# First loads of a hybrid decoder trunk: pieces of 256 and 768 weight columns between the input chunks, and the first norm's squares behind all operands

## The chip, the cores and the metric

The kernel runs on one core of one Trainium2 chip, as one launch. The metric is the device time of an execution in microseconds (us); lower is better. All times below are from the kernel's own runs or from the trace of one profiled execution of it.

In the profile PE is TensorE's matmuls and PEld its weight loads, DVE is VectorE, ACT is ScalarE, POOL is GpSimd, and SP is the queue that issues nearly all loads. L165 is line 165 of the kernel before.

## The reference

Two layers over x of 512 tokens and 1024 features, in float32. Layer 0 has a causal convolution module, layer 1 differential attention; each is followed by a SwiGLU feed-forward (2816 wide) and a gated per-layer embedding. What the change touches is the start of layer 0:

```python
def rms_norm(x, g):
    y = x * rsqrt(mean(x * x, axis=-1, keepdims=True) + EPS)
    return y * g

def conformer_conv(x, w_pw1, b_pw1, dw_w, dw_b, ln_g, ln_b, w_pw2, b_pw2):
    a = x @ w_pw1 + b_pw1                                 # (512, 2048)
    u = a[..., :1024] * sigmoid(a[..., 1024:])
    u = depthwise_causal_conv(u, dw_w, width=31) + dw_b   # each feature by itself
    u = silu(layer_norm(u, ln_g, ln_b))
    return u @ w_pw2 + b_pw2

u = rms_norm(h, conv_norm_g[0])
h = h + conformer_conv(u, ...)
```

## The kernel before

Activations lie transposed: 8 chunks `h[0]` to `h[7]` of 128 features (partitions) by 512 tokens, 256 KB each. A weight tile is 128 x 1024: the 8 input chunks' blocks of 128 x 128 side by side, for 128 output features; 512 KB each.

Every product runs as three matmuls (`mm3`, L163 to L167) on operands split in two: a high part, cast to the reduced-precision matmul type on ScalarE, and a low part, the rest, subtracted on VectorE. `weight()` (L146) takes the next tile from `wts` with a load on the SP queue into one of two `wraw` buffers, casts it into one of four `whi` (L158) and subtracts into one of four `wlo` (L160). A load into a `wraw` buffer waits until the tile before the last one has been cast and subtracted. In the text the tiles are called w0, w1, w2 and so on, in the order of their loads.

The norm is a class with two steps for a chunk. `operands(c)` makes the two matmul operands of h[c] times the gain (`A`: ScalarE at L179, VectorE at L180). `squares(c)` adds the chunk's squares into `acc` (ScalarE at L201 and L204, VectorE at L205). The scale by the root mean square is not in the operands: it is multiplied into the results. For that, `columns()` sums `acc` over the partitions on TensorE (L211), `rsqrt_cols` makes the reciprocal root of it on VectorE and GpSimd (L228, L230), `diagonal` spreads that over the identity (L235), a matmul with ones turns it into rows (L245), and ScalarE copies these to SBUF as `rb` (L220).

The convolution stage runs over 8 output chunks c. Each takes two weight tiles, a gate half and a value half, and each `half(w)` sums 8 input chunks x 3 matmuls = 24 matmuls in one accumulator. The accumulators (`mm`) are four PSUM buffers taken in turn: chunk 0 takes the first two, chunk 1 the other two, and chunk 2 needs the first again. VectorE reads an accumulator at L482 (gate) and L488 (value), times `rb`, and by that frees it. The depthwise convolution runs beside this on VectorE, GpSimd and, for some chunks in a phased layout, on TensorE (`pe_taps`).

At the start the SP queue loads w0 in two halves of 512 columns with h[0] between them, then w1's first half, h[1], w1's second half, h[2], and h[3] to h[7], the depthwise weights, w2, the side input `p` of layer 0 and w3. ScalarE and VectorE do the operands of a chunk and right behind them its squares. Nine matmuls on constants (`WARM`, L140) stand ahead of everything on TensorE.

The order on each engine is made by the framework's scheduler at build time, from the program's order and a model of the times; on the chip each engine runs its list in that order, and a wait holds up all that stands behind it.

Of the kernel before, what the change touches and what calls it, by code (L numbers as in the profile page):

```python
# [13 lines left out]
F32R = mybir.dt.float32r  # L14
AF = mybir.ActivationFunctionType
ALU = mybir.AluOpType
# [4 lines left out]
P = 128  # L21
S = 512
D = 1024
NC = D // P
# [22 lines left out]


SHIFT = 1
WARM = 9  # L50
ALONE = (7,)
CUTS = 2

# [39 lines left out]
def trunk(ctx, tc, xT, pT, wts, diag, dww, vec, rel, onehot, lamv, out):  # L93
    nc = tc.nc
    V, A, G, T = nc.vector, nc.scalar, nc.gpsimd, nc.tensor
# [7 lines left out]
    def sb(shape, tag, bufs, dt=F32):  # L103
        uid[0] += 1
        return pool.tile(shape, dt, tag=tag, name=f"{tag}_{uid[0]}", bufs=bufs)
# [10 lines left out]
    f = lambda ap: ap.bitcast(F32)  # L116
# [6 lines left out]
    def col(name, i=0):  # L123
        a, _ = VEC[name]
        return vt[:, a + i : a + i + 1]
# [12 lines left out]
    t = tp()  # L138
    for k in range(WARM):
        T.matmul(t[:, 0:P], ident, ones, start=True, stop=True)  # L140
# [2 lines left out]
    wnext = [0]  # L143
    loaded = [None]

    def weight(n=1024, pieces=1, between=(), eng=V, after=None, behind=None):  # L146
        i = wnext[0]
        wnext[0] += 1
        raw = sb([P, 1024], "wraw", 2)
        hi = sb([P, 1024], "whi", 4, F32R)  # L150
        lo = sb([P, 1024], "wlo", 4, F32R)
        for k in range(pieces):
            cut = slice(k * n // pieces, (k + 1) * n // pieces)
            loaded[0] = nc.sync.dma_start(raw[:, cut], wts[i, :, cut])
            if k < len(between):
                between[k]()
            with tc.issue_after(behind.ins) if behind else nullcontext():
                A.copy(hi[:, cut], raw[:, cut])  # L158
            with tc.issue_after(after.ins) if after else nullcontext():
                eng.tensor_tensor(lo[:, cut], raw[:, cut], f(hi[:, cut]), ALU.subtract)  # L160
        return hi, lo

    def mm3(acc, a, b, first, last):  # L163
        (ah, al), (bh, bl) = a, b
# [11 lines left out]
    h = [sb([P, S], f"h{c}", 1) for c in range(NC)]  # L176

    def split_scaled(src, scale, hi, lo):
        A.activation(hi, src, AF.Copy, scale=scale)  # L179
        V.scalar_tensor_tensor(lo, src, scale, f(hi), ALU.mult, ALU.subtract)  # L180

    class Norm:

# [9 lines left out]
        def operands(self, c):  # L193
            hi = sb([P, S], f"A{2 * c}", 1, F32R)
            lo = sb([P, S], f"A{2 * c + 1}", 1, F32R)
            split_scaled(h[c], col(self.g, c), hi, lo)
            self.u.append((hi, lo))

        def squares(self, c):
            if c == 0:  # L200
                A.activation(self.acc, h[c], AF.Square)  # L201
            else:
                sq = wk()
                self.square = A.activation(sq, h[c], AF.Square)  # L204
                self.last = self.eng.tensor_tensor(self.acc, self.acc, sq, ALU.add)  # L205
# [42 lines left out]

    norm = Norm("conv_g", V)
    def load(c):  # L250
        return lambda: nc.sync.dma_start(h[c], xT[c])

    w0 = weight(pieces=2, between=(load(0),))
    norm.operands(0)
    w1 = weight(pieces=2, between=(load(1), load(2)))
    pair_loads = [loaded[0]]
    pairs = [(w1, w0)]
    for c in range(3, NC):
        load(c)()
    dwt = sb([P, NC * KW], "C4", 2)  # L260
    nc.sync.dma_start(dwt, dww)
    for c in range(1, NC):
        norm.operands(c)
    pairs.append((weight(), weight())[::-1])
    pair_loads.append(loaded[0])
    for c in range(NC):
        norm.squares(c)

    def pfeatures(layer, parts):
        for k, (hi, lo) in enumerate(parts):  # L270
# [329 lines left out]
    norm = Norm("ffn_g0")  # L600
# [8 lines left out]
    def ffn(norm, after, space):  # L609
# [102 lines left out]
        def strassen(i):  # L712

            w = operands(i)

            def product(acc, name):
                for k in range(4):
                    mm3(acc, wpart(w[name], k), comb[name][k], k == 0, k == 3)

            one, two, three, four = sc(), mm(), mm(), tp()  # L720
            t, e, g = wk(), big(), big()
            first, second = slice(0, H2), slice(H2, S)
            product(one[:, first], 1)
            A.copy(t[:, first], one[:, first])
            A.mul(t[:, second], one[:, first], -1.0)
            product(three[:, first], 5)
            product(three[:, second], 7)
            product(two[:, first], 2)
            product(two[:, second], 6)
            V.tensor_tensor(e, two, t, ALU.add)  # L730
            V.tensor_tensor(
                g.rearrange("p (a s) -> p a s", a=2), three.rearrange("p (a s) -> p a s", a=2),
                e[:, second].unsqueeze(1).to_broadcast([P, 2, H2]), ALU.add,
            )
            V.tensor_tensor(e[:, second], three[:, second], g[:, first], ALU.add)
            product(four[:, second], 4)
            V.tensor_tensor(g[:, second], four[:, second], g[:, second], ALU.add)
            product(four[:, first], 3)
            V.tensor_tensor(g[:, first], four[:, first], g[:, first], ALU.subtract)
            return e, g  # L740
# [91 lines left out]
    norm = Norm("attn_g")  # L832
# [202 lines left out]
    def stage_o(hd):  # L1035
        t = tp()
        for i in range(4):
            T.transpose(t[:, i * P : (i + 1) * P], osb[hd][:, i * P : (i + 1) * P], ident)
        hi = sb([P, S], f"A{2 * hd}", 1, F32R)
        lo = sb([P, S], f"A{2 * hd + 1}", 1, F32R)  # L1040
        split_scaled(t, gains[:, 1:2], hi, lo)
        ot[hd] = (hi, lo)
# [9 lines left out]
    def take(n):  # L1052
        got, stages[:n] = [s for _, s in stages[:n]], []
        return got

    waiting = None
    for what, at, pace in QKV:
        ws = slab(GLO if what == "q" and at > 0 else 0, P * at[1] if what == "v" else S)
        for tb in range(4):
            if (what, at, tb) == ("v", (6, 2), 0):  # L1060
                ph = pfeatures(1, [both(sb([P, 2, S], t, 1, F32R)) for t in ("B0", "B1")])
            between = take(3 * pace[tb])
# [23 lines left out]
    for m in range(NC):  # L1086
        if m % 4 == 0:
            w = weight()
# [9 lines left out]
    norm = Norm("ffn_g1")  # L1098
# [149 lines left out]
```

## Time and profile before

| | |
|---|---|
| time, median of 3 runs | 1251.86 us (1250.25 to 1252.58) |
| time of the profiled execution | 1249.44 us |
| its span in the trace | 1247.7 us |
| instructions in the trace | 18537 |
| read from HBM | 151.91 MB |

A row of the timeline or of the waits gives start and duration in us, the engine, the source line, the operation, the tile written and the tiles read, and, in brackets, how long the engine had been idle and what ended it. Rows that follow each other on one engine can be merged (x2); then the duration is their sum. The page's busy time of TensorE holds pipelined matmuls, so it shows where TensorE waits, not how well it works.

### The profile page before, as it was taken

How to read it: one execution, taken by the hardware profiler on the slowest of the kernel's cores; microseconds unless marked ns; L12 is line 12 of the kernel's file. 1: busy time of each engine (PE TensorE's matmuls, PEld its weight loads, DVE VectorE, ACT ScalarE, POOL GpSimd, SP SyncE). 2: the span in 40 equal slices, each digit the busy share in tenths (PEclk: the TensorE clock that was granted, in tenths of full speed). 3: DMA queues.
4: the chain of work that ended last, by engine and by line, in shares of the span. 5: the costliest groups of instructions: out<-in, count | busy, mean ns of one | idle time of the engine just before them, and what ended most of it. 6: DMA issues, size and time to landing. Idle time of an engine off the chain costs nothing.

```text
span 1247.7 us, 18537 instructions
## 1 busy us (share of the span) xinstructions
PE 1234.6 (99%) x7152; PEld 1083.8 (87%) x7152; DVE 885.6 (71%) x1422; ACT 614.1 (49%) x1023; POOL 264.4 (21%) x231
## 2 busy tenths in 40 slices
PE   9999999999999999999999999999999999999998
PEld 7888788898899889988888988878898999899887
DVE  6998765965688568677667879546964598458665
ACT  6743454542355325355557778635432355235441
POOL 2852522000000000042526644131000000000030
PEclk9999999999999999999999999999999999999999
DMA  8666223464466444243232215122654466443241
GB/s 300 201 195 189 67 73 113 125 172 127 127 176 179 128 125 124 64 142 95 85 111 76 75 45 159 62 87 82 185 141 131 119 175 185 130 120 110 76 136 68
DMA packets 60598, 158.39 MB, mean 127 GB/s; under 512 B 6452, under 2 KB 11060, under 8 KB 60509
## 3 DMA queue, kind: packets, MB, share of 16 engines
q1 hardware_dynamic: 53776, 136.99, 34.6%
q0 software_dynamic: 4608, 16.78, 7.9%
q10 hardware_dynamic: 2124, 3.43, 0.9%
q8 instruction: 56, 0.92, 0.3%
q14 instruction: 34, 0.27, 0.1%
HBM read 151.91 MB, written 4.21 MB: 125 GB/s over the span
## 4 chain that ended last, share of the span: by engine, by line
PE 95%; DVE 3%; ACT 1%; issue 1%; DMA 0%; SPq 0%; DVEq 0%; ACTq 0%
PE mm L165 25%; PE mm L166 25%; PE mm L167 25%; PE tp L166 2%; PE tp L167 2%; PE tp L165 2%; PE sc L371 2%; PE sc L166 1%; PE sc L167 1%; PE sc L165 1%; PE mm L1012 1%; PE mm L371 1%; PE tp L998 1%; PE sc L979 1%; PE mm L327 1%
## 5 line engine op out<-in xcount | busy, mean ns | idle before, releaser
L166 PE MATMUL mm<-A,whi 128*128 128x512 f32 (+1 forms) x904 | 311.4, 346 | 1.1 <-DVE A L576 0.9
L167 PE MATMUL mm<-A,whi 128*128 128x512 f32 (+1 forms) x904 | 310.2, 343 | 0.0
L165 PE MATMUL mm<-A,wlo 128*128 128x512 f32 (+1 forms) x904 | 306.8, 345 | 3.2 <-DVE wlo L160 1.7
L158 ACT CAST whi<-wraw 128x1024 fp32r<-128x1024 f32 (+2 forms) x150 | 151.1, 1014 | 226.2 <-PE mm L167 94.1
L160 DVE TENSOR_TENSOR wlo<-wraw,whi 128x1024 fp32r<-128x1024 f32 (+2 forms) x147 | 186.0, 1268 | 64.5 <-ACT whi L158 64.0
L165 PEld LDWEIGHTS mm<-A,wlo 128*128 128x128 f32 x904 | 171.4, 190 | 24.3 <-ACT A L179 2.3
L166 PEld LDWEIGHTS mm<-A,whi 128*128 128x128 f32 x904 | 171.5, 190 | 23.0 <-DVE A L576 1.8
L167 PEld LDWEIGHTS mm<-A,whi 128*128 128x128 f32 x904 | 171.5, 190 | 20.7 <-issue 1.4
L167 PE MATMUL mm<-B,whi 128*128 128x512 f32 x368 | 143.4, 391 | 0.0
L166 PE MATMUL mm<-B,whi 128*128 128x512 f32 x368 | 143.4, 391 | 0.0
L165 PE MATMUL mm<-B,wlo 128*128 128x512 f32 x368 | 141.4, 392 | 0.0
L685 POOL DMA_DIRECT2D C<-in_wts x32 | 28.1, 878 | 512.4 <-DVE h L796 178.9
L205 POOL TENSOR_TENSOR acc<-acc,wk 128x512 f32<-128x512 f32 x35 | 56.2, 1606 | 219.0 <-ACT wk L204 113.3
L167 PEld LDWEIGHTS mm<-B,whi 128*128 128x128 f32 x368 | 69.2, 188 | 14.9
L165 PE MATMUL mm<-whi,A 128*128 128x512 f32 (+1 forms) x224 | 81.5, 367 | 0.0
L166 PE MATMUL mm<-wlo,A 128*128 128x512 f32 (+1 forms) x224 | 81.5, 366 | 0.0
L166 PEld LDWEIGHTS mm<-B,whi 128*128 128x128 f32 x368 | 69.2, 188 | 14.2
L165 PEld LDWEIGHTS mm<-B,wlo 128*128 128x128 f32 x368 | 69.1, 188 | 14.1
L167 PE MATMUL mm<-whi,A 128*128 128x512 f32 (+1 forms) x224 | 81.2, 364 | 0.0
L796 DVE TENSOR_TENSOR h<-mm,h 128x512 f32<-128x512 f32 x48 | 33.0, 687 | 64.7 <-PE mm L167 64.7
L230 POOL TENSOR_TENSOR r<-v,mhalf 128x8 f32<-128x8 f32 (+1 forms) x31 | 46.7, 1505 | 104.7 <-DVE v L228 100.3
L678 DVE TENSOR_TENSOR wlo<-wraw,whi 128x1024 fp32r<-128x1024 f32 x32 | 39.2, 1224 | 31.3 <-ACT whi L677 31.1
(269 smaller groups left out, 2618.5 us busy)
## 6 DMA issues: line engine op xcount, KB each, us to landing
wraw<-in_wts SPq DMA_DIRECT2D x162, 512.0 KB, 3.6
C<-in_wts SPq DMA_DIRECT2D x32, 512.0 KB, 4.5
C<-in_wts POOLq DMA_DIRECT2D x32, 512.0 KB, 6.2
bias<-in_wts SPq DMA_DIRECT2D x32, 256.0 KB, 3.4
wraw<-in_wts SPq DMA_DIRECT2D x16, 384.0 KB, 3.1
D<-in_diag SPq DMA_DIRECT2D x22, 256.0 KB, 4.6
C<-in_diag SPq DMA_DIRECT2D x16, 256.0 KB, 4.7
h<-in_xT SPq DMA_DIRECT2D x8, 256.0 KB, 5.1
```

Of the source, the lines that this page charges most:

```text
L158: A.copy(hi[:, cut], raw[:, cut])
L160: eng.tensor_tensor(lo[:, cut], raw[:, cut], f(hi[:, cut]), ALU.subtract)
L165: T.matmul(acc, al, bh, start=first, stop=False)
L166: T.matmul(acc, ah, bl, start=False, stop=False)
L167: return T.matmul(acc, ah, bh, start=False, stop=last)
L205: self.last = self.eng.tensor_tensor(self.acc, self.acc, sq, ALU.add)
L230: last_pow[0] = G.tensor_tensor(r[:, :n], v[:, :n], mhalf[:, :n], ALU.pow)
L327: last_tap[0] = T.matmul(acc, dg[:, j % 4], ups[c][:, j : j + S], start=(j == 0), stop=(j == PE_TAPS[c] - 1))
L371: last_tap[0] = T.matmul(acc[:, g * P : (g + 1) * P], w, ups[c][:, g, LEAD - m : LEAD - m + P], start=(m == 0), stop=(m == LAGS - 1),)
L678: V.tensor_tensor(lo, raw, f(hi), ALU.subtract)
L685: nc.gpsimd.dma_start(q, wts[i + 2].rearrange("p (a s) -> p a s", a=2), accum_op=ALU.add)
L796: V.tensor_tensor(h[m], acc, h[m], ALU.add)
```

## The change

The code of `weight()` is taken apart into `opened()`, which takes the buffers, and `fetch()`, which loads, casts and subtracts a range of columns. w0 and w1 are opened together, and the first loads are: 256 columns of w0, h[0], 256 columns of w1, h[1], the other 768 of w0, h[2], the other 768 of w1, then h[3] to h[7]. A first piece of 256 columns is what input chunks 0 and 1 multiply. All squares of the first norm are ordered behind the cast of the last operand. One matmul on constants is left out (`WARM` 9 to 8). The arithmetic is the same.

```diff
--- before.py
+++ after.py
@@ -47,7 +47,7 @@
 
 
 SHIFT = 1
-WARM = 9
+WARM = 8
 ALONE = (7,)
 CUTS = 2
 
@@ -143,22 +143,23 @@
     wnext = [0]
     loaded = [None]
 
-    def weight(n=1024, pieces=1, between=(), eng=V, after=None, behind=None):
+    def opened():
         i = wnext[0]
         wnext[0] += 1
-        raw = sb([P, 1024], "wraw", 2)
-        hi = sb([P, 1024], "whi", 4, F32R)
-        lo = sb([P, 1024], "wlo", 4, F32R)
-        for k in range(pieces):
-            cut = slice(k * n // pieces, (k + 1) * n // pieces)
-            loaded[0] = nc.sync.dma_start(raw[:, cut], wts[i, :, cut])
-            if k < len(between):
-                between[k]()
-            with tc.issue_after(behind.ins) if behind else nullcontext():
-                A.copy(hi[:, cut], raw[:, cut])
-            with tc.issue_after(after.ins) if after else nullcontext():
-                eng.tensor_tensor(lo[:, cut], raw[:, cut], f(hi[:, cut]), ALU.subtract)
-        return hi, lo
+        return i, sb([P, 1024], "wraw", 2), sb([P, 1024], "whi", 4, F32R), sb([P, 1024], "wlo", 4, F32R)
+
+    def fetch(w, cut, eng=V, after=None, behind=None):
+        i, raw, hi, lo = w
+        loaded[0] = nc.sync.dma_start(raw[:, cut], wts[i, :, cut])
+        with tc.issue_after(behind.ins) if behind else nullcontext():
+            A.copy(hi[:, cut], raw[:, cut])
+        with tc.issue_after(after.ins) if after else nullcontext():
+            eng.tensor_tensor(lo[:, cut], raw[:, cut], f(hi[:, cut]), ALU.subtract)
+
+    def weight(n=1024, **how):
+        w = opened()
+        fetch(w, slice(0, n), **how)
+        return w[2:]
 
     def mm3(acc, a, b, first, last):
         (ah, al), (bh, bl) = a, b
@@ -176,8 +177,9 @@
     h = [sb([P, S], f"h{c}", 1) for c in range(NC)]
 
     def split_scaled(src, scale, hi, lo):
-        A.activation(hi, src, AF.Copy, scale=scale)
+        cast = A.activation(hi, src, AF.Copy, scale=scale)
         V.scalar_tensor_tensor(lo, src, scale, f(hi), ALU.mult, ALU.subtract)
+        return cast
 
     class Norm:
 
@@ -193,8 +195,8 @@
         def operands(self, c):
             hi = sb([P, S], f"A{2 * c}", 1, F32R)
             lo = sb([P, S], f"A{2 * c + 1}", 1, F32R)
-            split_scaled(h[c], col(self.g, c), hi, lo)
             self.u.append((hi, lo))
+            return split_scaled(h[c], col(self.g, c), hi, lo)
 
         def squares(self, c):
             if c == 0:
@@ -248,23 +250,28 @@
 
     norm = Norm("conv_g", V)
     def load(c):
-        return lambda: nc.sync.dma_start(h[c], xT[c])
-
-    w0 = weight(pieces=2, between=(load(0),))
-    norm.operands(0)
-    w1 = weight(pieces=2, between=(load(1), load(2)))
+        nc.sync.dma_start(h[c], xT[c])
+
+    w0, w1 = opened(), opened()
+    start, rest = slice(0, 2 * P), slice(2 * P, NC * P)
+    for c, (w, cut) in enumerate(((w0, start), (w1, start), (w0, rest))):
+        fetch(w, cut)
+        load(c)
+        norm.operands(c)
+    fetch(w1, rest)
     pair_loads = [loaded[0]]
-    pairs = [(w1, w0)]
+    pairs = [(w1[2:], w0[2:])]
     for c in range(3, NC):
-        load(c)()
+        load(c)
     dwt = sb([P, NC * KW], "C4", 2)
     nc.sync.dma_start(dwt, dww)
-    for c in range(1, NC):
-        norm.operands(c)
+    for c in range(3, NC):
+        cast = norm.operands(c)
     pairs.append((weight(), weight())[::-1])
     pair_loads.append(loaded[0])
-    for c in range(NC):
-        norm.squares(c)
+    with tc.issue_after(cast.ins):
+        for c in range(NC):
+            norm.squares(c)
 
     def pfeatures(layer, parts):
         for k, (hi, lo) in enumerate(parts):
```

The scheduler places what follows anew. Three places are shown, each before and after; the kernel after has other line numbers (L158 is L155 there, L160 L157, L165 to L167 are L166 to L168, L179 is L180, L201 L203, L204 L206, L211 L213, L228 L230, L235 L237, L245 L247, L279 L286 and L482 L489).

The first place is ScalarE at the end of the first norm's operands: `A` are operands, `wk` squares, `wth` and `wtl` the side input, and `whi` behind `wraw` the weight w2. Before:

```order
L179 ACTIVATE A_33_143<-h_12_91,vec_63 128x512
L204 ACTIVATE wk_180<-h_12_91 128x512
L179 ACTIVATE A_35_147<-h_13_92,vec_63 128x512
L204 ACTIVATE wk_183<-h_13_92 128x512
L179 ACTIVATE A_37_151<-h_14_93,vec_63 128x512
L204 ACTIVATE wk_186<-h_14_93 128x512
L158 CAST whi_156<-wraw_155 128x1024
L279 CAST wth_256<-B_66_260 128x512
L279 CAST wtl_258<-B_66_260 128x512
```

Now:

```order
L180 ACTIVATE A_37_150<-h_14_92,vec_63 128x512
L203 ACTIVATE acc_93<-h_7_85 128x512
L206 ACTIVATE wk_167<-h_8_86 128x512
L206 ACTIVATE wk_170<-h_9_87 128x512
L206 ACTIVATE wk_173<-h_10_88 128x512
L206 ACTIVATE wk_176<-h_11_89 128x512
L286 CAST wth_255<-B_66_259 128x512
L286 CAST wtl_257<-B_66_259 128x512
L206 ACTIVATE wk_179<-h_12_90 128x512
L155 CAST whi_155<-wraw_154 128x1024
L206 ACTIVATE wk_182<-h_13_91 128x512
```

The squares were between the operands and w2 came right behind the last of them; now six squares and the side input stand between the last operand and w2's cast.

The second place is TensorE around the column sums of the norm, which write `tp` from `acc`. Before (the first rows are the end of chunk 0, `mm_286` is the gate half of chunk 1):

```order
L166 MATMUL mm_227<-A_38_152,whi_110 128x512
L167 MATMUL mm_227<-A_37_151,whi_110 128x512
L211 MATMUL tp_216<-ones_70,acc_94 128x1 x4
L165 MATMUL mm_286<-A_19_105,wlo_157 128x512
L166 MATMUL mm_286<-A_20_106,whi_156 128x512
```

Now (`mm_285` is the gate half of chunk 1, `mm_311` its value half):

```order
L167 MATMUL mm_285<-A_38_151,whi_155 128x512
L168 MATMUL mm_285<-A_37_150,whi_155 128x512
L213 MATMUL tp_215<-ones_70,acc_93 128x1 x4
L166 MATMUL mm_311<-A_22_104,wlo_162 128x512
L167 MATMUL mm_311<-A_23_105,whi_161 128x512
```

The column sums have moved behind 24 more matmuls, a whole half. The matmul that spreads the diagonal (L245) stood within chunk 1's value half, behind 8 of its 24 matmuls; now it stands behind all of them, and the next matmul is the first of chunk 2, `mm_420`.

The third place is what ScalarE and VectorE do around `rb` and the first read of an accumulator (`whi_275` and `wlo_276` before, `whi_274` and `wlo_275` now, are w4; the next tiles are w5 and w6). ScalarE before:

```order
L158 CAST whi_162<-wraw_161 128x1024
L158 CAST whi_275<-wraw_274 128x1024
L220 COPY rb_252<-tp_253 128x512
L158 CAST whi_281<-wraw_280 128x1024
L483 ACT_TABLE_LOAD
```

ScalarE now, down to the copy of `rb`, with two more casts ahead of it:

```order
L155 CAST whi_161<-wraw_160 128x1024
L155 CAST whi_274<-wraw_273 128x1024
L155 CAST whi_280<-wraw_279 128x1024
L155 CAST whi_409<-wraw_408 128x1024
L222 COPY rb_251<-tp_252 128x512
```

VectorE before, from the root's first step (`v`) on:

```order
L228 TENSOR_SCALAR v_56_221<-tp_216 128x4
L235 TENSOR_TENSOR wk_225<-ident_65,r_57_223 128x512
L160 TENSOR_TENSOR wlo_276<-wraw_274,whi_275 128x1024
L482 TENSOR_TENSOR big_266<-mm_191,rb_252 128x512
L488 TENSOR_TENSOR big_267<-mm_227,rb_252 128x512
```

VectorE now, from the same step on, with two more subtractions ahead of the first read of an accumulator (`mm_190`):

```order
L230 TENSOR_SCALAR v_56_220<-tp_215 128x4
L237 TENSOR_TENSOR wk_224<-ident_65,r_57_222 128x512
L157 TENSOR_TENSOR wlo_275<-wraw_273,whi_274 128x1024
L157 TENSOR_TENSOR wlo_281<-wraw_279,whi_280 128x1024
L157 TENSOR_TENSOR wlo_410<-wraw_408,whi_409 128x1024
L489 TENSOR_TENSOR big_265<-mm_190,rb_251 128x512
```

The copy of `rb` stood behind w4's cast and now stands behind those of w4, w5 and w6; the first read of an accumulator stood behind w4's subtraction and now stands behind those of w4, w5 and w6.

On the SP queue the side input's load now stands ahead of w2's, and one of two later loads (256 KB, for the feed-forward) has moved up ahead of w3. Behind the convolution stage the order is that of before.

## The prediction

> **What bounds the kernel now.** I read the page's shares and its chain first, then the busy times by stretch, then the timeline of the first 32 us.
>
> ```profile
> PE 1234.6 (99%) x7152; PEld 1083.8 (87%) x7152; DVE 885.6 (71%) x1422; ACT 614.1 (49%) x1023; POOL 264.4 (21%) x231
> PE 95%; DVE 3%; ACT 1%; issue 1%; DMA 0%; SPq 0%; DVEq 0%; ACTq 0%
> ```
>
> TensorE is busy for 99% of the span and is 95% of the chain that ended last. The stretches (columns: stretch, length, PE busy and count, PEld, DVE, ACT, POOL, granted clock, DMA share, GB/s) say where it is not:
>
> ```profile
> 30.00:100.00 70.00, 70.00 (x382) 60.36 (x381) 68.53 (x81) 39.68 (x55) 45.44 (x34) 1.00 0.59 187
> 100.00:200.00 100.00, 98.58 (x502) 80.34 (x501) 69.55 (x91) 50.16 (x76) 38.23 (x27) 1.00 0.39 118
> 200.00:1200.00 1000.00, 995.48 (x5942) 884.61 (x5941) 703.17 (x1188) 491.94 (x847) 169.01 (x155) 1.00 0.43 120
> ```
>
> From 30 to 100 us there is no gap at all, and 1.42 us up to 200. So whatever TensorE gains or loses before 30 us is kept to the end: nothing behind it is waiting for something else that could take it up. The change touches only this opening and, through it, the order of the convolution stage. The opening on TensorE (with the copies it waits for):
>
> ```profile
> 1.50 4.21 PE L140 MATMUL tp<-ones,ident 128*128 128x128 f32 x18 [1.50 <-POOL ident masks.py:199]
> 4.80 0.72 ACT L179 ACTIVATE A<-h,vec 128x512 fp32r<-128x512 f32 x1
> 5.58 0.29 PEld L165 LDWEIGHTS mm<-A,wlo 128*128 128x128 f32 x1 [0.16 <-ACT A L179]
> 5.58 0.62 PE L165 MATMUL mm<-A,wlo 128*128 128x512 f32 x1
> 6.36 0.19 PEld L166 LDWEIGHTS mm<-A,whi 128*128 128x128 f32 x1 [0.50 <-DVE A L180]
> 7.81 0.73 PE L165 MATMUL mm<-A,wlo 128*128 128x512 f32 x2 [0.71 <-ACT A L179]
> ...
> 18.09 0.39 PE L167 MATMUL mm<-A,whi 128*128 128x512 f32 x1
> 18.31 0.95 PE L211 MATMUL tp<-ones,acc 128*128 128x1 f32 x8
> 19.12 0.49 PE L165 MATMUL mm<-A,wlo 128*128 128x512 f32 x1
> 19.45 0.40 PE L166 MATMUL mm<-A,whi 128*128 128x512 f32 x1
> ...
> 26.29 0.39 PE L166 MATMUL mm<-A,whi 128*128 128x512 f32 x1
> ...
> 31.05 0.39 PE L165 MATMUL mm<-A,wlo 128*128 128x512 f32 x1
> ```
>
> The first real matmul starts at 5.58. From 19.45 to 26.29 there are 30 matmuls, so one takes 0.228 us. The 48 of channel chunk 0 need 10.9 us and take 12.7 (5.58 to 18.31): only some 1.8 us of waiting is there to be had. Then come the column sums of the norm (L211, 0.81 us of TensorE), and the 97th matmul, the first that needs a used PSUM accumulator again, at 31.05.
>
> **The first pieces.** One load follows another: h0 is in at about 4.75 (it is read from 4.80), and h7 is worked out below to land at 11.7. Between them lie 2560 KB, so 0.70 us for 256 KB. The first piece of w0 shrinks from 256 to 128 KB, so h0 lands 0.35 us earlier and the first matmul starts at 5.23. That rows half as long move at this pace no row shows: the bounds are 0 (a half piece takes as long) and 0.7; I take 0.35. One warm-up matmul less ends the warm-up at 1.50 + 8/9 of 4.21 = 5.24, just then. The 17th matmul is the first that needs the rest of w1: this is in at 4.75 + 0.70 x (1792 - 512)/256 = 8.25, its cast takes about 0.83 and its subtraction 0.95 (between the rows of 512 and of 1024 columns), so it starts at 10.1, and the 48th ends 32 x 0.228 later, at 17.4. **The opening gains 0.9 us** (18.31 before).
>
> **What is late next: w2.** The 49th matmul starts with the low half of w2, which ScalarE casts and VectorE subtracts behind the squares:
>
> ```profile
> 3.53 3.23 SPq L251 DMA_DIRECT2D h<-in_xT  x6
> ...
> h<-in_xT SPq DMA_DIRECT2D x1, 256.0 KB, 5.3
> ...
> 14.38 0.71 ACT L179 ACTIVATE A<-h,vec 128x512 fp32r<-128x512 f32 x1
> 14.99 0.62 ACT L204 ACTIVATE wk<-h 128x512 f32<-128x512 f32 x1
> 15.51 1.04 ACT L158 CAST whi<-wraw 128x1024 fp32r<-128x1024 f32 x1
> 16.46 0.61 ACT L279 CAST wth<-B 128x512 fp32r<-128x512 f32 x1
> 16.97 0.62 ACT L279 CAST wtl<-B 128x512 fp32r<-128x512 f32 x1
> 17.26 1.21 DVE L160 TENSOR_TENSOR wlo<-wraw,whi 128x1024 fp32r<-128x1024 f32 x1
> ...
> 18.58 2.11 DVE L160 TENSOR_TENSOR wlo<-wraw,whi 128x1024 fp32r<-128x1024 f32 x1
> ```
>
> The last of the six issues starts at 3.53 + 3.23 - 0.33 = 6.43 (0.33 is one issue) and lands 5.3 us later: h7 is there at 11.7, with the same bytes ahead of it as before. Before, ScalarE reached A of h7 only at 14.38, since it did a square after each; now it waits for h7 itself. From 11.75 on its new order is: A of h7 (0.61 to the next start), five squares (0.52 each), two casts of the side input (0.51 each), another square, the cast of w2 (1.04): 11.75 + 0.61 + 2.6 + 1.02 + 0.52 + 1.04 = 17.55. The side input now loads ahead of w2, which costs w2 1.4 us of landing (14.85 for about 13.4); it hides behind these squares. The subtraction takes 1.21 (first row) or 2.11 (second row, beside GpSimd's subtractions of the side input, which now lie at the same place). I take the middle, 1.66, as either neighbour fits: **the 49th matmul starts at 19.3 (18.85 to 19.75)**, 1.9 us after the 48th ended. Before it stood at 19.12 with the column sums already paid; now they are still to come. The gain of the opening is gone, and 1.0 us with it.
>
> **What takes the place of it: the accumulators.** There are four `mm` accumulators, and the 97th matmul takes the first again. It waits until VectorE has read it with rb (L482), and rb hangs on the column sums. Before, these came after 48 matmuls and L245 in the middle of the fourth sum; now they come after 72 and 96. The chain, from the rows of before:
>
> ```profile
> 20.61 0.15 DVE L228 TENSOR_SCALAR v<-tp 128x4 f32<-128x4 f32 x1
> 21.80 1.02 POOL L230 TENSOR_TENSOR r<-v,mhalf 128x4 f32<-128x4 f32 x1
> 22.86 0.69 DVE L235 TENSOR_TENSOR wk<-ident,r 128x512 f32<-128x512 f32 x1 [2.10 <-POOL r L230]
> 25.59 1.05 ACT L158 CAST whi<-wraw 128x1024 fp32r<-128x1024 f32 x1 [7.04 <-DMA wraw<-in_wts]
> 26.52 1.02 PE L245 MATMUL tp<-wk,ones 128*128 128x512 f32 x2
> 26.67 1.23 DVE L160 TENSOR_TENSOR wlo<-wraw,whi 128x1024 fp32r<-128x1024 f32 x1 [3.12 <-ACT whi L158]
> 27.58 0.59 ACT L220 COPY rb<-tp 128x512 f32<-128x512 f32 x1 [0.94 <-PE tp L245]
> 27.93 0.33 SPq L154 DMA_DIRECT2D wraw<-in_wts  x1
> 28.19 0.69 DVE L482 TENSOR_TENSOR big<-mm,rb 128x512 f32<-128x512 f32 x1 [0.30 <-ACT rb L220]
> ...
> 26.68 0.86 PE tp L245 x2
> ...
> wraw<-in_wts SPq DMA_DIRECT2D x1, 512.0 KB, 3.7
> ```
>
> Three things that were apart before now stand in a row. VectorE subtracts w4 only behind the diagonal (L235). The load of w6 takes w4's buffer, so it is issued when that subtraction ends (26.67 + 1.23 = 27.90; issue at 27.93), and a load of 512 KB into a quiet queue lands 3.7 us later. And rb's copy now stands on ScalarE behind the cast of w6, and L482 on VectorE behind its subtraction. Counted from the start of the column sums: 0.95 for them, 0.15 v, 1.02 r, 0.62 until the next VectorE start, 1.23 subtraction of w4, 3.7 load of w6, 1.04 cast, 1.22 subtraction (rb's copy lies beside it), 0.62 L482 behind it, and 0.3 for eight hand-overs of 0.03 to 0.05: **10.85 us**. TensorE's cover is 0.81 for the sums, 24 x 0.228 of the fourth sum and 0.86 of L245 (its piece in the chain that ended last): **7.15 us**. It stands still for 3.7. w4 itself lands as before (cast at 25.59, well before the diagonal ends at about 27.7), behind the same bytes.
>
> So the 97th matmul starts at 19.3 + 24 x 0.228 + 10.85 = 35.6, against 31.05: **+4.55 us**. The bounds are those of w2 (0.45 each way) and 0.5 each way of the chain, 3.6 to 5.5. The later moves (loads of w8 and w9 ahead of the phased input, taps five matmuls earlier) I cost at nothing: VectorE, too, starts its taps some 4.4 us later for equal work, so it falls no further behind than TensorE.
>
> **The clock.** TensorE does not stand still for 3.7 us anywhere before. The only longer rest is at the end:
>
> ```profile
> 1242.80:1244.90 2.10, 0.07 (x1) 0.00 (x0) 1.27 (x3) 0.42 (x1) 0.00 (x0) 1.00 0.14 47
> 1244.90:1245.00 0.10, 0.00 (x0) 0.00 (x0) 0.00 (x0) 0.00 (x0) 0.00 (x0) 0.59 0.00 0
> ```
>
> The last matmul ends at 1242.87, and some 2.05 us later the granted clock falls to a half. The first rows show the way back: TensorE works from 1.50, a weight load still takes 0.29 at 5.58 and 0.19 at 6.36, so full speed came after 4.1 to 4.9 us. If the stall of 3.7 us does what the rest of 2.05 us did, 4.4 us of matmuls run at half pace and 2.2 us more are lost. The bounds are 0 (the clock holds) and 2.4 + 2.4, if w2's wait of 1.9 us costs the clock too.
>
> The Trainium skill (TensorE: Matmul & The Clock Gate, "What's actually happening") makes the clock fall after an idle window of about 3.4 us that runs free of the kernel. By it, a stall of 3.7 us would mostly not hold a whole window, and the sum would be +4.55 instead of +6.75. The trace differs: its clock fell after 2.05 us.
>
> **The sum.** +4.55 + 2.2 = +6.75 us. The profiled execution took 1249.44 (1.74 more than its span), so it would be 1256.2; the runs' median is 1251.86, 2.4 above that execution, and on it the forecast is **1258.6**.
>
> **The rivals.**
> - The stall comes, but the clock holds: +4.55, 1256.4. For it speaks TensorE's longest wait behind the opening, which cost no clock (its row among the waits: total, times, longest):
>
> ```profile
> PE mm L165 <- DVE wlo L160: 1.7, 1, 1.7
> ```
>
> - Part is won back. TensorE idles 1.42 us between 100 and 200; if it waits there for loads, which don't move, the lag shrinks by as much: +3.1, 1255.0. A chain shorter by another 1 us, if w6 lands sooner, gives 1254. Against it: what it waits for there is VectorE's and ScalarE's work, which lags as well.
> - The other side: both new waits fail to bind, and the opening's 0.9 stays, 1251.0. It decides at 7.15 us for the chain (10.85 by my sum) and 17.4 for w2's low half (19.3). It needs ScalarE and VectorE not to take the casts in the order built, or w6 to be there 3.7 us sooner. Only if the first pieces land at their best (0.7) and the gaps before the 17th matmul go as well does it come near -2.5 us.
> - The change doesn't do what it says: the squares slip between the operands after all. The order built has them behind; I give this nothing of its own.
>
> **How the numbers follow.** The forecast has 0.44, the stall with full clock 0.33, part won back 0.12, no stall 0.11. A measurement of this kernel tells about 0.2% (2.5 us) from no change. No stall gives 0.03 faster and 0.08 same, half of part won back is same: faster 0.03, same 0.14, slower 0.83. The range leaves out the no-stall case and the worst of the clock: from +1.4 (part won back, at its best) to +10 (both waits cost the clock): 1253.2 to 1261.8.
>
> **What would show it.** Right: a gap of about 1.9 us on TensorE at 17.4, ended by the subtraction of w2; another of 3 to 4.5 us at about 32, ended by L482, with the cast of w6 just ahead of rb's copy and waiting for its load; a granted clock below 1.00 in the next 5 us, with matmuls at some 0.45 us; and from there the same stage lengths as before. Wrong: no gap at 32, or one that a later gap of before takes up; a first matmul not before 5.58.

## The result and the profile after

The changed kernel takes 1260.88 us (median of 4 runs, 1259.63 to 1262.93) beside 1251.28 us for the kernel before (4 runs): a ratio of 1.0073, 95% interval 1.006 to 1.0086. It is **9.6 us slower**; the forecast was 1258.6, range 1253.2 to 1261.8. The profiled execution took 1262.93 us, with a span of 1261.1. Of all executions one, of e2 below, ran in a slow state (5914 us) and is left out of its ratio.

The page's shares and the chain that ended last, after the change:

```profile
PE 1240.8 (98%) x7150; PEld 1086.9 (86%) x7150; DVE 884.8 (70%) x1422; ACT 614.9 (49%) x1023; POOL 260.1 (21%) x231
PE 91%; DVE 3%; DMA 3%; ACT 1%; issue 1%; SPq 0%; POOL 0%; DVEq 0%; ACTq 0%; POOLq 0%
```

TensorE still bounds the kernel, but its part of the chain has fallen from 95 to 91%, and a load that nothing waited for before stands in it with 3%. The stretches (columns as before the change: stretch, length, PE, PEld, DVE, ACT, POOL, granted clock, DMA share, GB/s) say where:

```profile
17.00:22.00 5.00, 2.53 (x12) 1.78 (x11) 4.82 (x4) 3.65 (x6) 2.81 (x2) 1.00 1.05 405
22.00:30.00 8.00, 8.00 (x34) 6.56 (x33) 2.09 (x4) 2.09 (x2) 0.01 (x1) 0.79 0.53 174
30.00:36.00 6.00, 6.00 (x26) 4.41 (x24) 2.96 (x3) 0.00 (x0) 1.02 (x1) 1.00 0.30 91
36.00:40.00 4.00, 0.55 (x3) 0.33 (x3) 2.25 (x3) 2.73 (x4) 0.00 (x0) 1.00 0.58 197
40.00:44.00 4.00, 4.00 (x12) 3.13 (x11) 4.00 (x6) 3.21 (x5) 0.00 (x0) 0.57 0.58 145
...
100.00:200.00 100.00, 98.55 (x502) 80.31 (x501) 72.06 (x93) 44.94 (x67) 38.50 (x28) 1.00 0.36 112
200.00:1200.00 1000.00, 994.39 (x5927) 883.48 (x5927) 698.83 (x1184) 493.07 (x849) 167.63 (x154) 1.00 0.43 120
```

There are two holes in TensorE's work, at 17 to 22 and at 36 to 40 us, and behind each of them a stretch with a clock below full (0.79 and 0.57). From 100 us on the stages are as busy as before (98.55 of 100 us, 98.58 before; 994.39 of 1000, 995.48 before). TensorE's timeline gives the two holes as waits:

```profile
4.99 0.80 PE L166 MATMUL mm<-A,wlo 128*128 128x512 f32 x1
...
18.70 0.39 PE L168 MATMUL mm<-A,whi 128*128 128x512 f32 x1
21.55 0.50 PE L166 MATMUL mm<-A,wlo 128*128 128x512 f32 x1 [2.47 <-DVE wlo L157]
...
28.77 0.95 PE L213 MATMUL tp<-ones,acc 128*128 128x1 f32 x8
...
35.16 1.02 PE L247 MATMUL tp<-wk,ones 128*128 128x512 f32 x2
39.63 0.50 PE L166 MATMUL mm<-A,wlo 128*128 128x512 f32 x1 [3.45 <-DVE big L489]
```

The 48th matmul starts at 18.70. The 49th waits for the low half of w2 until 21.55, the 97th until 39.63 for VectorE to free an accumulator (31.05 before): 8.58 us late. The 24 matmuls from 21.55 to 28.77 take 7.22 us instead of 24 x 0.228 = 5.47. Comparing the start of the same instruction in both traces, the lag is 10.32 us from 75 us on and stays there up to 385 us.

Before each hole, ScalarE, VectorE, GpSimd and the SP queue did this (timeline; the rows of the first and the second hole; the row of five adds at 14.70 holds the two at 17.08 and 18.78):

```profile
12.86 0.71 ACT L180 ACTIVATE A<-h,vec 128x512 fp32r<-128x512 f32 x1
14.70 5.67 DVE L207 TENSOR_TENSOR acc<-acc,wk 128x512 f32<-128x512 f32 x5
16.08 0.60 ACT L286 CAST wth<-B 128x512 fp32r<-128x512 f32 x1
16.58 0.61 ACT L286 CAST wtl<-B 128x512 fp32r<-128x512 f32 x1
16.76 1.37 POOL L287 TENSOR_TENSOR wth<-B,wth 128x512 fp32r<-128x512 f32 x1 [15.24 <-ACT wth L286]
17.08 1.60 DVE L207 TENSOR_TENSOR acc<-acc,wk 128x512 f32<-128x512 f32 x1
17.64 1.04 ACT L155 CAST whi<-wraw 128x1024 fp32r<-128x1024 f32 x1
18.09 1.72 POOL L287 TENSOR_TENSOR wtl<-B,wtl 128x512 fp32r<-128x512 f32 x1
18.78 1.58 DVE L207 TENSOR_TENSOR acc<-acc,wk 128x512 f32<-128x512 f32 x1
20.29 1.21 DVE L157 TENSOR_TENSOR wlo<-wraw,whi 128x1024 fp32r<-128x1024 f32 x1
...
31.06 0.69 DVE L237 TENSOR_TENSOR wk<-ident,r 128x512 f32<-128x512 f32 x1 [1.14 <-POOL r L232]
31.66 2.35 DVE L157 TENSOR_TENSOR wlo<-wraw,whi 128x1024 fp32r<-128x1024 f32 x2
32.91 1.46 SPq L153 DMA_DIRECT2D wraw<-in_wts  x2
36.67 1.04 ACT L155 CAST whi<-wraw 128x1024 fp32r<-128x1024 f32 x1 [7.24 <-DMA wraw<-in_wts]
37.62 0.58 ACT L222 COPY rb<-tp 128x512 f32<-128x512 f32 x1
37.75 1.23 DVE L157 TENSOR_TENSOR wlo<-wraw,whi 128x1024 fp32r<-128x1024 f32 x1 [3.73 <-ACT whi L155]
38.89 0.68 DVE L489 TENSOR_TENSOR big<-mm,rb 128x512 f32<-128x512 f32 x1
```

First hole: the side input's two casts stand ahead of w2's on ScalarE. The cast of w2 ends at 18.68, but its subtraction starts only at 20.29: VectorE still has the fifth add of the squares ahead of it. The first three of the five adds take 0.68 to 0.69 us each, as before. The last two take 1.60 and 1.58, because GpSimd works on the side input's low halves at the same time: each of them ends 0.55 us behind the end of a GpSimd subtraction (18.13 and 19.81). At 0.69 us each they would have ended at about 18.6 (an estimate), just before the cast of w2 does. Second hole: the load of w6 goes out at 32.91, ScalarE waits for it with its cast until 36.67, and the copy of rb, whose input is there since 36.18, stands behind that cast until 37.62. L489 comes at 38.89 behind w6's subtraction.

### The profile page after: what moved, and what is told of

It reads as the page before. It is cut to its first block, busy times and chain, and to the rows that moved or that the text cites. A ratio compares the mean times of both kernels' runs of the same rounds, so it can differ in the third digit from the quotient of the medians.

```text
span 1261.1 us, 18535 instructions
## 1 busy us (share of the span) xinstructions
PE 1240.8 (98%) x7150; PEld 1086.9 (86%) x7150; DVE 884.8 (70%) x1422; ACT 614.9 (49%) x1023; POOL 260.1 (21%) x231
## 4 chain that ended last, share of the span: by engine, by line
PE 91%; DVE 3%; DMA 3%; ACT 1%; issue 1%; SPq 0%; POOL 0%; DVEq 0%; ACTq 0%; POOLq 0%
PE mm L166 25%; PE mm L167 24%; PE mm L168 24%; PE tp L168 2%; PE tp L167 2%; PE tp L166 2%; PE sc L378 2%; DMA wraw<-in_wts 2%; PE mm L1019 1%; PE sc L167 1%; PE sc L168 1%; PE sc L166 1%; DMA C<-in_wts 1%; DVE wlo L157 1%; PE mm L378 1%
## 5 line engine op out<-in xcount | busy, mean ns | idle before, releaser
L166 PE MATMUL mm<-A,wlo 128*128 128x512 f32 (+1 forms) x904 | 309.3, 347 | 9.8 <-DVE wlo L157 5.1
L167 PE MATMUL mm<-A,whi 128*128 128x512 f32 (+1 forms) x904 | 312.0, 346 | 1.1 <-DVE A L583 1.0
L168 PE MATMUL mm<-A,whi 128*128 128x512 f32 (+1 forms) x904 | 310.8, 344 | 0.0
L155 ACT CAST whi<-wraw 128x1024 fp32r<-128x1024 f32 (+2 forms) x150 | 151.2, 1014 | 236.3 <-DMA wraw<-in_wts 100.5
L157 DVE TENSOR_TENSOR wlo<-wraw,whi 128x1024 fp32r<-128x1024 f32 (+2 forms) x147 | 186.4, 1271 | 64.0 <-ACT whi L155 63.8
L166 PEld LDWEIGHTS mm<-A,wlo 128*128 128x128 f32 x904 | 172.0, 191 | 33.3 <-DVE wlo L157 5.2
L167 PEld LDWEIGHTS mm<-A,whi 128*128 128x128 f32 x904 | 172.3, 191 | 23.3 <-DVE A L583 1.8
L168 PEld LDWEIGHTS mm<-A,whi 128*128 128x128 f32 x904 | 172.1, 190 | 20.8 <-issue 1.0
L167 PE MATMUL mm<-B,whi 128*128 128x512 f32 x368 | 143.3, 390 | 0.0
L168 PE MATMUL mm<-B,whi 128*128 128x512 f32 x368 | 143.3, 390 | 0.0
L166 PE MATMUL mm<-B,wlo 128*128 128x512 f32 x368 | 141.3, 392 | 0.0
L168 PEld LDWEIGHTS mm<-B,whi 128*128 128x128 f32 x368 | 69.1, 188 | 15.1
L166 PE MATMUL mm<-whi,A 128*128 128x512 f32 (+1 forms) x224 | 81.5, 366 | 0.0
L167 PE MATMUL mm<-wlo,A 128*128 128x512 f32 (+1 forms) x224 | 81.4, 365 | 0.0
L167 PEld LDWEIGHTS mm<-B,whi 128*128 128x128 f32 x368 | 69.1, 188 | 14.1
L166 PEld LDWEIGHTS mm<-B,wlo 128*128 128x128 f32 x368 | 69.1, 188 | 14.1
L168 PE MATMUL mm<-whi,A 128*128 128x512 f32 (+1 forms) x224 | 81.1, 364 | 0.0
```

The source lines that it names most:

```text
L166: T.matmul(acc, al, bh, start=first, stop=False)
L167: T.matmul(acc, ah, bl, start=False, stop=False)
L168: return T.matmul(acc, ah, bh, start=False, stop=last)
```

## The experiments

All of them are variants of the changed kernel or of the kernel before, each timed beside the kernel before on the same chip (its medians there 1251.5 us in 21 runs for e1 to e4, 1251.75 in 29 for e5 to e7). The theory: two orders that the scheduler builds, the side input ahead of w2 and rb behind w6, make the two holes, and each hole costs the clock besides.

### e1: the holes filled with constant matmuls

The changed kernel with 9 matmuls on constants behind the 48th, and 11 behind the matmuls that spread the norm; the next gate's sum is ordered behind them.

```diff
+    def filler(n, after):
+        t = sc()
+        with tc.issue_after(after.ins):
+            for _ in range(n):
+                last = T.matmul(t[:, 0:P], ident, ones, start=True, stop=True)
+        return tc.issue_after(last.ins)
...
-            pg = half(wg)
+            with filler(FILL[c], last_half[0] if c == 1 else spreading) if c < 3 else nullcontext():
+                pg = half(wg)
```

> The changed kernel with matmuls on constants in TensorE's two gaps: 9 behind the 48th matmul (some 2.1 us of the 2.5 us gap ahead of w2's low half) and 11 behind the matmul that spreads the diagonal (some 2.6 us of the 3.4 us gap ahead of the 97th). They add work and take no wait away. Theory, the clock: the 24 matmuls behind each gap are slow because the rest costs TensorE its clock. Then both stretches run at 0.228 us a matmul with the granted clock at 1.00, the gaps end where they did, and 1.8 + 1.7 us come back: about 3.5 us below the changed kernel, 6 us above before. Rival: the matmuls behind the gaps are slow for another reason (operands or accumulators that come late): nothing comes back, 9.6 us above before. Second rival: the dummies lie in the way: slower than the change.

Measured: 1269.28 us, ratio 1.0139 (1.0124 to 1.0154). TensorE's timeline and the stretches of e1:

```profile
18.81 2.17 PE L324 MATMUL sc<-ones,ident 128*128 128x128 f32 x18
21.48 0.50 PE L167 MATMUL mm<-A,wlo 128*128 128x512 f32 x1 [0.50 <-DVE wlo L158]
...
37.56 0.50 PE L167 MATMUL mm<-A,wlo 128*128 128x512 f32 x1 [0.64 <-DVE big L501]
```

```profile
22.00:30.00 8.00, 8.00 (x40) 6.71 (x40) 2.91 (x6) 2.09 (x2) 1.03 (x1) 1.00 0.57 188
...
60.00:100.00 40.00, 36.03 (x183) 30.11 (x184) 34.08 (x43) 22.10 (x32) 23.53 (x21) 0.91 0.59 187
100.00:200.00 100.00, 95.91 (x483) 78.09 (x482) 68.57 (x89) 44.48 (x66) 39.99 (x29) 0.98 0.36 107
```

Up to 44 us this shows what it was made for. The 49th matmul starts at the same time as in the changed kernel (21.48 for 21.55), since it waits for the same subtraction; but the clock stays at 1.00, and the 97th comes at 37.56 instead of 39.63. The convolution's matmuls between 34 and 40 us of the kernel before lag by 6.7 us instead of 10.3: 3.6 us are back, where 3.5 were expected. The total shows nothing of this: the added matmuls moved the scheduler's order of the taps, and TensorE waits anew (4.0 us of 60 to 100 us, with the clock down to 0.91), so that the lag grows to 18.6 by 125 us. Against the expectation the total is 8.4 us above the changed kernel's, and gives no price for the clock.

### e2: rb copied ahead of w6's cast

```diff
-            A.copy(r, spread(self.dg))
+            self.copied = A.copy(r, spread(self.dg))
...
-            pairs.append((weight(), weight())[::-1])
+            pairs.append((weight(behind=norm.copied if c == 2 else None), weight())[::-1])
```

> The changed kernel with w6's cast ordered behind the copy of rb: that copy and the first read of an accumulator then stand behind w5 instead of w6 on ScalarE and VectorE; all else keeps its place. Theory, the chain of accumulators: the 97th matmul waits for w6's load, cast and subtraction. Without them rb's copy follows the spreading matmul (which ends at 36.0), so 0.65 of copy and 0.7 of the read later, at 37.4 instead of 39.6, the 97th starts; the gap of 1.4 us costs no clock, so 2.2 + 1.7 = 3.9 us come back: 5.7 us above before. The first gap and its clock stay. Rival: another late thing (w5, or the diagonal) holds the read as well: no more than 1 us comes back, 8.6 to 9.6 us above before.

Measured: 1257.59 us, ratio 1.0033 (1.0019 to 1.0047). TensorE's waits between 5 and 60 us in e2 (total, times, longest) and its stretches:

```profile
PE mm L166 <- DVE wlo L157: 2.9, 2, 2.5
PE mm L166 <- DVE big L489: 1.4, 1, 1.4
```

```profile
22.00:30.00 8.00, 8.00 (x34) 6.58 (x33) 1.59 (x3) 2.10 (x2) 0.66 (x1) 0.80 0.52 174
...
40.00:44.00 4.00, 4.00 (x19) 3.32 (x18) 4.00 (x6) 3.52 (x6) 0.80 (x1) 1.00 0.79 246
```

The second hole is 1.4 us instead of 3.45, and the clock behind it holds; the first hole (2.5) and its loss (0.80) remain. The lag at 125 us is 6.02 instead of 10.32, so 4.3 us are gone: 2.05 of waiting and 1.74 of clock, the rest in the opening. The order of rb and w6 on ScalarE makes the second hole.

### e3: the squares alone, e4: the pieces alone

e3 is the kernel before, its old loads and nine warm-up matmuls, with only the squares ordered behind all operands. e4 is the changed kernel with the squares left to the scheduler:

```diff
-    with tc.issue_after(cast.ins):
-        for c in range(NC):
-            norm.squares(c)
+    for c in range(NC):
+        norm.squares(c)
```

> The kernel before, with only the squares ordered behind all operands; loads, pieces and warm-up as before. The scheduler then again puts the column sums behind 72 matmuls and the spreading one behind 96, but w2's cast ahead of the side input's and rb's copy behind w5, not w6. Theory, order not squares as such: the late sums cost only a gap of some 1.4 us at the 97th matmul (copy of rb and first read), no clock is lost, and the opening gains some 0.9: within 1 us of before. Rival, the squares carry the loss: 8 to 10 us above before. Between them, 3 to 5 us above, if w2's low half is still late by 1 us or more and the clock goes once.

> The changed kernel with the squares left where the scheduler puts them (one behind each operand, as before); pieces of 256 and 768 columns and the warm-up as changed. The column sums stand behind 48 matmuls again. Theory: the pieces alone cost only the slower loads of the opening (the 48th matmul 0.6 us later than before) and no clock: 0 to 1.5 us above before. Rival, the pieces carry the loss (their late loads make w2 late by themselves): 5 to 10 us above before. Second rival: without the late sums the earlier first matmul shows as a gain of 0.5 to 1 us.

Measured: e3 1253.89 us, ratio 1.0016 (1.0006 to 1.0025); e4 1253.12 us, ratio 1.0011 (1.0001 to 1.002). TensorE's longest wait between 5 and 60 us in e3, and then in e4:

```profile
PE mm L165 <- DVE big L484: 1.4, 1, 1.4
```

```profile
PE mm L166 <- ACT wk L206: 2.0, 1, 2.0
```

By the medians e3 costs 2.4 us and e4 1.6, and both parts together 9.6. With the squares alone the scheduler casts w2 ahead of the side input and copies rb ahead of w6, so the hole at the 97th matmul is 1.4 us. With the pieces alone there is no hole there at all; instead TensorE waits 2.0 us, up to 10.66, for the 768 columns of w0: ScalarE waits for their load until 8.69, and VectorE subtracts them until 10.51 (the square that the row names is only what ended last). Either lost one stretch of clock in the opening (0.90 over the first 17 us), which was expected of neither: both totals lie above what was expected. The loss is therefore not the sum of the two parts: it comes from the order that the scheduler builds when it is given both.

### e5: the side input behind w2

```diff
-            A.copy(hi[:, cut], raw[:, cut])
+            casts.append(A.copy(hi[:, cut], raw[:, cut]))
...
-            A.copy(hi, raw)
+            with tc.issue_after(casts[4].ins) if layer == 0 else nullcontext():
+                A.copy(hi, raw)
```

> The changed kernel with the side input's two casts ordered behind the cast of w2. The scheduler then also puts the copy of rb behind w5's cast instead of w6's. Theory (both gaps come from the order on ScalarE and what VectorE gets from it, and each gap of over about 1.6 us costs a clock window of 1.75 us): the 49th matmul starts 1.2 to 2.2 us sooner than 21.55, the gap at the 97th falls from 3.6 to about 1.4 as with rb ahead of w6, no or one clock window is lost before 50 us, the lag behind the kernel before at 100 us is 2 to 4 us instead of 10.3, and the total is 1253 to 1256 (ratio 1.001 to 1.004). Rival (the late loads of the opening set the 49th matmul, whatever the order): the 49th stays at 21 or later, a clock window is lost behind it, the total is that of the kernel with rb alone moved, about 1257.5.

Measured: 1253.68 us, ratio 1.0013 (1.0005 to 1.0022). The timeline of e5 at both places:

```profile
15.24 3.08 DVE L208 TENSOR_TENSOR acc<-acc,wk 128x512 f32<-128x512 f32 x4
17.19 1.04 ACT L156 CAST whi<-wraw 128x1024 fp32r<-128x1024 f32 x1
18.26 1.22 DVE L158 TENSOR_TENSOR wlo<-wraw,whi 128x1024 fp32r<-128x1024 f32 x1
18.83 1.81 POOL L289 TENSOR_TENSOR wth<-B,wth 128x512 fp32r<-128x512 f32 x1 [17.31 <-ACT wth L288]
19.40 4.28 DVE L208 TENSOR_TENSOR acc<-acc,wk 128x512 f32<-128x512 f32 x3
19.54 0.50 PE L167 MATMUL mm<-A,wlo 128*128 128x512 f32 x1
...
33.95 0.50 PE L167 MATMUL mm<-A,wlo 128*128 128x512 f32 x1 [1.40 <-DVE big L491]
```

Only the two casts' place is given, and the loads are those of the changed kernel: 7.2 of the 9.6 us are gone (1253.68 for 1260.88). The 49th matmul starts at 19.54, 2.0 us sooner, with no wait ahead of it. Four adds take 3.08 us, w2's subtraction comes right behind its cast, and the two adds that GpSimd stretches (1.79 and 1.59 us of the row of three) come after it, where nobody waits for them. The second hole is 1.4 us, since the scheduler now copies rb ahead of w6, and the clock does not fall before 100 us. It came up late, though: the first rise to full clock is at 10.80 us in this trace and at 4.36 to 7.03 in the others, and from 8.2 us until then matmuls follow each other at 0.43 us. (The granted clock of a stretch reads 1.00 there, since the trace has no record of it before its first rise.) The 48th matmul starts at 19.26, 0.56 later than in the changed kernel, and this hides a wait of about that length: w2's low half is ready at 19.49. The lag that remains at 100 us is 3.03. The rival, that the late loads of the opening set the 49th matmul whatever the order, falls: the loads were no earlier here.

### e6 and e7: pieces of 512 and 512 columns, alternating

Both have the one edit below; e6 keeps the squares behind all operands, e7 leaves them to the scheduler as in e4.

```diff
-    start, rest = slice(0, 2 * P), slice(2 * P, NC * P)
+    start, rest = slice(0, 4 * P), slice(4 * P, NC * P)
```

> The changed kernel with pieces of 512 and 512 columns in place of 256 and 768, in the same alternating order, with the squares behind all operands; the first matmul's weight piece is then twice as large. ScalarE casts w2 ahead of the side input here and copies rb behind w5. Theory (the uneven pieces slow the opening's loads, the order of casts makes the gaps): first matmul about 0.3 us later than with 256 columns, the load of w0's rest done by 7 us instead of 7.8, h7 by 12.2 instead of 12.9, the 48th matmul ends before 18.6, gaps under 1.6 us and no clock window lost before 50 us, total 1251.5 to 1254. Rival (the pieces' size does not matter, only the number of transfers ahead of a chunk): the last chunk lands at 12.7 or later and the 48th matmul ends at 18.9 or later; total 1254 to 1257.

> Pieces of 512 and 512 columns alternating with the chunks of the input, and the squares placed by the scheduler as in the kernel before, so that a square stands behind each operand's cast on ScalarE. Here the side input is cast ahead of w2 as in the changed kernel, and rb is copied behind w5 and ahead of w6 as in the kernel before. Theory (the squares behind the operands are what delay the column sums, the uneven pieces what slows the loads): no gap over 1 us at the 97th matmul, the lag at 100 us between -0.5 and +1.5 us, total 1250.5 to 1253. Rival (the alternating order itself costs, since w0's second piece comes behind w1's first): a wait of 1 to 2 us for w0's second piece at 7 to 10 us as with 256 and 768 columns, a clock window lost, total 1253 or more.

Measured: e6 1252.58 us, ratio 1.0008 (1.0 to 1.0016); e7 1252.72 us, ratio 1.0006 (0.9998 to 1.0015). TensorE's timeline in e6, and then in e7:

```profile
18.05 0.50 PE L166 MATMUL mm<-A,wlo 128*128 128x512 f32 x1 [0.44 <-DVE wlo L157]
...
32.48 0.50 PE L166 MATMUL mm<-A,wlo 128*128 128x512 f32 x1 [1.40 <-DVE big L489]
```

```profile
18.71 0.95 PE L213 MATMUL tp<-ones,acc 128*128 128x1 f32 x8
...
109.20 4.26 PE L377 MATMUL sc<-C,D 128*128 128x128 f32 x36 [0.90 <-DMA C<-pi]
```

In e6 the scheduler, too, casts w2 first and copies rb ahead of w6, so it tells of the pieces and of the order together. It starts the 49th matmul at 18.05, ahead of the kernel before (19.12), but its column sums are still to come, and 1.4 us at the 97th matmul give it back. e7 has no wait at the 97th matmul, as expected. It was also expected within 1.5 us of the kernel before at 100 us. It was so up to 64 us (0.97), but at 100 us the lag was 2.05 and by 120 us 3.2: new waits of 0.4 and 0.2 us at 66 and 75 us and of 0.9 us at 109 us, the last two for a chunk in the phased layout, are a part of it; the rest was not followed. No variant is faster than the kernel before.

The load pace of the opening can be read across all traces: GB/s from 3.0 to 5.6 us, and the mean time of a packet of 2 KB (one row of 512 columns) that starts between 4 and 6 us:

```
pieces of w0 and w1, order          GB/s          2 KB packet, ns
512 + 512, before and e3            359, 344      87, 100
512 + 512 alternating, e6, e7       338, 307      92, 105
256 + 768, after, e1, e2, e4, e5    263, 267,     125, 132, 133,
                                    266, 272,     111, 156
                                    248
```

With 256 and 768 columns the queue moves about a fifth less in this time: 248 to 272 GB/s in five traces, 307 to 359 in the four others. The small pieces themselves went at nearly full pace (1 KB packets in 47 to 50 ns between 2 and 6 us); it is the packets of the chunks behind them that take longer. Why is open.

## Why the prediction was right, and where it was off

- **What bounds the kernel: right.** What TensorE lost before 45 us was kept. It idles 1.45 us from 100 to 200 us, as before, so the rival that wins part back there falls; the lag at 125 and at 301 us is the same 10.32.
- **The first matmul: right.** Forecast 5.23, measured 4.99. That is 0.59 us of the 0.7 that the bounds allowed, but one pair of traces says little: with a first piece of 256 columns the first matmul starts at 4.88 to 5.22 in five traces, with 512 columns at 5.34 to 5.72 in four.
- **The rest of the loads: mis-sized, and this step turned the opening's sign.** The sum took one pace, 0.70 us for 256 KB, and had w1's 768 columns in at 8.25; the cast that waits for them started at 9.64. From there ScalarE works without a rest, reaches A of h7 at 12.86 instead of 11.75, and the 48th matmul starts at 18.70 where the forecast had it end at 17.4. The opening loses 0.6 us instead of gaining 0.9. The bounds on this term covered the first half piece alone, not the pace of the pieces behind it.
- **w2's low half: the right wait, too short.** Forecast 19.3 (18.85 to 19.75), measured 21.55. Of the 2.25 us, 1.13 are the late cast (18.68 for 17.55), which is the load pace. The subtraction starts 1.61 us behind the cast's end, and it then takes 1.21 us with 0.05 of hand-over instead of 1.66 and 0.09, which wins 0.49 back. The 1.61 was not in the sum: it priced the subtraction beside GpSimd, but not the adds of squares queued ahead of it on VectorE, which GpSimd stretched. Nor do its two rows part the cases: in the kernel before, a subtraction of GpSimd (17.16 to 19.60) lay beside the one of 1.21 us too. The Trainium skill (SBUF — State Buffer, "SBUF: two separate sides") has VectorE's operations with two SBUF inputs and GpSimd's lock each other out for whole instructions. This trace agrees: 0.68 us for an add alone, 1.60 and 1.58 beside GpSimd's two subtractions, and 1.79 and 1.59 in e5.
- **The chain to the 97th matmul: right.** Forecast 10.85 us from the column sums on, measured 28.77 to 39.63, 10.86; the stall 3.7, measured 3.45. e2 and e5 show its cause, since with rb copied ahead of w6 it is 1.4.
- **The clock: the right mechanism, counted once instead of twice.** Forecast one loss of 2.2 us behind the second hole, with a second loss as the upper bound; measured are 1.75 behind the first hole (7.22 for 5.47) and 1.74 behind the second (the lag grows from 8.58 to 10.32). That the clock holds through a hole, the strongest rival, is refuted for both. One loss costs 1.75 us and not 2.2, because half pace lasts 3.41 us and not 4.4. With e1, which fills the holes with work, the clock stays at 1.00 up to 61 us, and with e5, whose only hole is 1.4 us, from its first rise up to 785 us.

The sum, on the profiled executions: 39.63 - 35.6 = 4.03 us more at the 97th matmul (2.25 for w2, 1.75 for the clock, 0.03 for the chain and rounding), less 0.46, since the loss of clock behind it is 1.74 and not 2.2; +6.75 forecast and 3.57 more make the measured 10.32. The range held this only because its upper end had been given a second loss of clock. The runs' medians differ by 9.6. The two profiled executions differ by more, 13.49 us, because the clock took another 1.7 us in attention from the one after and none from the one before. This is chance, as the last section argues; of the four executions of the changed kernel two had a mean granted clock of 0.995 (the profiled one among them) and took 1262.3 us on average, and two had 0.997 and took 1259.8. A further 0.7 us each at 385 to 398 us and at 776 to 800 us was not followed.

## What to carry over

When a change moves loads or ties down some instructions, the scheduler rebuilds the order around them, so each engine's rows have to be read again at every place where TensorE waits; here two neighbours that swapped places cost more than both intended edits (7.2 of 9.6 us came back by giving w2's cast its old place, with which the scheduler gave the copy of rb its own). Price a wait with all that stands ahead of it in its engine's queue, stretched by whatever the neighbouring engine does at that moment. And on an engine whose clock follows its use, reckon that a hole of 2 us or more can cost about 1.75 us again.

## What the hardware showed that was not expected

The trace records the granted clock's changes. Below are stretches at half clock, with TensorE's busy time in the 3.41 us ahead of each; the last row has two windows, by their ends, behind which the clock held:

```
kernel   half clock, us    PE busy in the 3.41 us ahead
after    23.02 to 26.44    1.47
after    40.09 to 43.50    0.46
after    794.44 to 797.85  1.95
e2       21.86 to 25.28    0.92
e3       7.77 to 11.18     1.99
e4       12.26 to 15.67    1.39
e5       785.62 to 789.03  1.97
held: e5 at 34.69 (2.01), e6 at 33.96 (2.01)
```

Each lasts 3.41 us (one in e1 twice that), and in one trace they lie a whole multiple of 3.41 us apart. So the clock is decided window by window, on a grid that stands elsewhere in each trace. The Trainium skill (TensorE: Matmul & The Clock Gate, "What's actually happening") gives such a free-running window of 3413 ns, and the traces agree. It also has the clock fall after at least one idle window; here windows with up to 2.01 of their 3.41 us at work fell. Between 4 and 50 us those with up to 1.99 us of work did and those with 2.01 or more did not. That is no rule for the whole kernel: at about 786 us windows with 1.84 to 2.01 fell in e2 to e6, while one with 1.68 that ended at 829 us held in e6, so the profile's busy time is not quite what decides. Where the grid cuts a hole in two, both halves can hold: attention's hole near 780 us cost the kernel before nothing (2.46 and 2.45 us of work in the two windows), and a window in seven of the eight others.

That this also makes differences between executions of one kernel is not shown by a trace, since each kernel has one. The runs fit it: of 29 executions of the kernel before, the five with a mean granted clock of 1.000 took 1250.9 us on average, the three with 0.996 or less 1254.2.
